# A hybrid decoder step on one core: convolution taps, mixers' weight loads and new latents moved in trace order

## The chip, the cores and the metric

The kernel runs on 1 core of one Trainium2 chip. The metric is the device time of one execution in microseconds (us). Before the change the median of 3 runs is 1201.39 us (1199.27 to 1204.67).

## The reference, cut to what matters

One layer of a decoder is computed for a prompt group (1 x 512 tokens and 16 learned meta tokens, 528 rows) and a sample group (8 sequences of 4 new tokens, 32 rows), with shared weights:

```python
h = x + 0.5 * swiglu(rmsnorm(x, ffn1_norm), ...)
z = rmsnorm(h, mix_norm) @ w_in          # -> q latent 256 | kv latent 256 | rope key 32 | conv input 2 x 512
a  = attention(q_lat, q_rope, c_kv, k_rope, w_uv)      # 8 heads over a compressed latent of 256
cv = silu(layernorm(depthwise_conv31(conv_in_a * sigmoid(conv_in_b)) + conv_b))
h = h + concat(rmsnorm(a), rmsnorm(cv)) @ w_out
h = h + 0.5 * swiglu(rmsnorm(h, ffn2_norm), ...)
```

Prompt attention is causal over the 528 rows. Each sample sequence attends to 4096 cached positions (32 pages of 128, found by a page table) and to its 4 new rows. The convolution is depthwise over 512 channels with 31 taps. The outputs are y of both groups, the new kv latents and rotary keys, and the last 30 rows of the convolution's input.

## The kernel before, in words

All activations are kept transposed, features on the 128 partitions and tokens (up to 560) along the free axis. A weight matrix streams in tiles; each is split into a high and a low part (`w_split`: ScalarE copies `wh` at L286, GpSimd subtracts `wl` at L287; where an FFN uses sums of weight blocks, VectorE subtracts at L300), and a product is made of three matmuls (`mm3`, L349).

On the chip the stages follow one another: the first FFN (to about 418 us), the input projections of the mixers (about 420 to 590), sample attention in 32 chunks of pages (about 446 to 733), prompt attention in 16 units (4 head pairs x 4 query tiles, about 591 to 731), the output projection (from about 741 to 787, first the convolution's four column groups, then attention's four), and the second FFN to the end. The convolution runs beside these: its taps from 460 to 640, its tail (mean, squares, norm, swish, second norm, split) from 640 to 741.

**How the order is made.** The kernel is written as coroutines that a small planner runs (`spawn`, `run`, L382 to 418). The planner has a clock of its own, in planned microseconds. A coroutine that yields a number advances this clock for everyone (0.715 for one `mm3` group of the projections, 1.6 for the scores of a chunk, 0.45 for its transposes, 1.05 for its products with the values). One that yields `Sleep(x)` is only not run before x has passed. One that yields an event waits for it. Where several can go on, the lowest priority number goes first: the convolution and the norms have 0, the two prompt workers 2, the main program 5. So the planner decides in which order instructions are traced. The framework then places each engine's instructions by readiness, with the traced order as priority, and from it come the order of each engine's queue and the buffers.

**Buffers.** Tiles of one tag share a set of buffers. The tag "t" has 10 (`Tm`): the probabilities `pr` and transposed probabilities of the prompt units, the squares `sq`, the tiles `th`, `cg`, `ot` are all of it. The rsqrt's work tiles "r" and "rr" have 1 each, its spread result "rb" 2. In PSUM the norms' sums take the banks "nr" and "cv". Weights' raw tiles `wr` have 3.

**The places of the change.**
- `conv_proc` (L917 for a tap): for each of 4 blocks of 128 channels, 31 operations on VectorE, one per tap, with a sleep of `TAP_PACE` after each; then ScalarE copies the sum to `acc` (L920) and GpSimd adds it to the sum over channels (L930). After the last block it spawns `conv_tail`.
- `conv_tail` (from L934): sleep `CS_LAT` (1.73); two halves of the mean on TensorE (L938), subtracted on VectorE (L941); four squares (L512) on ScalarE; sleep `CN_LAT` (8.16); a norm (`rsqrt_proc`: matmuls with ones L430, sqrt L462 and Newton's steps on VectorE L463 to L466, spread by L481, L483 and L485); per block the product by the norm (L953), tanh, bias, product (L958) and a square; sleep `CN_LAT` again; a second norm (its rsqrt on VectorE alone, L451 to L456); per block the product by gain and norm (L875) and the split into `mix` (L880 on ScalarE, L881 on GpSimd). Then `conv_done` is set.
- `w_split` and `w_dma` (L268 issues the load on SP's queue): after the split of tile j, loads are traced up to tile j + 4. A load waits in SP's queue until its buffer is free, that is until L287 has used the tile three loads earlier. SP also issues the page loads of the sample chunks (L1011).
- `latents_out` (L1497): when the scaled kv latents (`cc`, L818) are there, it stores them (L1501), transposes the samples' new latents on TensorE (L1504), copies them (L1505, L1506) and sets `new_ev`. `sample_proc` waits for `new_ev` at its chunk number 9 (L1144), for the scores against the new rows.
- `attn_norm` (from L1534): when the prompt workers and sample attention are done, four squares (L512, `sq<-at`), sleep 3.71, a norm, and the split of attention's half.
- The main program then waits for `conv_done` and does the convolution's half of the output projection for all 8 column groups, waits for attention's norm and does its half.

The planner's waits in these places, for reference:

```python
def rsqrt_proc(...):
    r0 = rsqrt(...)
    yield 0.3
    yield Sleep(RS_LAT)          # 4.05
    ...
    spread(rb, r0, site)
    yield 0.95
    ev.set(rb)
```

Of the kernel before, what the change touches and what calls it, by code (L numbers as in the profile page):

```python
# [52 lines left out]
CS_LAT = 1.73  # L53
CN_LAT = 8.16
AN_LAT = 3.71
TAP_PACE = 0.75

PAGE_TIME = 6.62

# [51 lines left out]
def kernel(  # L111
# [42 lines left out]
    def U(tag, shape, dt=F32, name="u"):  # L154
        return arena.tile(shape, dt, tag=tag, bufs=slots[tag], name=name)
# [24 lines left out]
    def SS(shape, name="ss", who="mm"):  # L180
        return ps_s.tile(shape, F32, tag=BANK_OF[who], bufs=BANKS[BANK_OF[who]], name=name)
# [29 lines left out]
    stream = []  # L211
# [3 lines left out]
    def add_w(ap, n):  # L215
        stream.append((ap, n))

    def add_ffn(gu, dn, apart=0, plain=NF):
        f0 = 0
        for nf in GROUPS:  # L220
            for f in range(f0, f0 + nf):
                if f == plain:
                    first_new.add(len(stream))
                add_w(gu[f], 2048 if f < plain else 0)
            for d in range(KD - (apart if f0 + nf == NF else 0)):
                add_w(dn[d, :, 128 * f0:128 * (f0 + nf)], 128 * nf)
            f0 += nf

    add_ffn(f1_gu, f1_d, 0, PLAIN1)
    for c in PLAN:  # L230
        for ap, n in {"q": [(w_in_t[0], 1024), (w_in_t[1], 1024)], 
                      "k": [(w_in_t[2], 1024)], "l": [(w_in_t[3], 1024)], "r": [(w_r_t, 512)],
                      "u": [(w_uq_t[0], 1024), (w_uq_t[1], 1024)]}.get(c) or [(w_in_t[4 + int(c, 16)], 1024)]:
            add_w(ap, n)
    add_w(w_uk_t, 1024)
    add_w(w_uv_t, 1024)
    for d, e in [(d, 1) for d in range(KD)] + [(d, 0) for d in range(KD)]:
        add_w(w_out_t[d, :, 512 * e:512 * e + 512], 512)
    add_ffn(f2_gu, f2_d, 2, PLAIN)


    subs = []
# [12 lines left out]
    def w_dma(upto):  # L255
        while st["dma"] < min(upto, len(subs)):
            i, c0, n = subs[st["dma"]]
            if n == 0:
                if c0 == 0:
                    raws[i, "a"] = []  # L260
                    for kh in range(2):
                        t = U("y" if i in first_new else "x", [128, 2, 512], F32, "ra")
                        nc.sync.dma_start(out=t, in_=stream[i][0][:, 1024 * kh:1024 * kh + 1024])
                        raws[i, "a"].append(t)
                st["dma"] += 1
                continue
            t = wpool.tile([128, n], F32, tag="wr", bufs=3, name="wr")
            nc.sync.dma_start(out=t, in_=stream[i][0][:, c0:c0 + n])  # L268
            raws[st["dma"]] = t
            dma_free[0] = max(dma_free[0], clock[0]) + n * WEIGHT_TIME  # L270
            st["dma"] += 1

    def w_split(upto):
        while st["split"] < min(upto, len(subs)):
            j = st["split"]
            n = subs[j][2]
            w_dma(j + 1)
            if n == 0:
                splits[j] = seven(*subs[j][0:2])
                st["split"] += 1  # L280
                w_dma(j + 8)
                continue
            raw = raws.pop(j)
            hi = wpool.tile([128, n], F32R, tag="wh", bufs=3, name="wh")
            lo = wpool.tile([128, n], F32R, tag="wl", bufs=3, name="wl")
            nc.scalar.activation(out=hi, in_=raw, func=AF.Copy)  # L286
            nc.gpsimd.tensor_tensor(out=lo, in0=raw, in1=hi.bitcast(F32), op=ALU.subtract)  # L287
            splits[j] = (hi, lo)
            st["split"] += 1
            w_dma(j + 4)  # L290

    def seven(i, m):

        a = raws[i, "a"]
        (a11, a21), (a12, a22) = [[t[:, j] for j in range(2)] for t in a]
        w = {0: a11, 4: a11, 5: a12, 6: a22}[m] if m in (0, 4, 5, 6) else raws[i, "s"]
        hi = wpool.tile([128, 512], F32R, tag="wh", bufs=3, name="wh")
        lo = wpool.tile([128, 512], F32R, tag="wl", bufs=3, name="wl")
        nc.scalar.activation(out=hi, in_=w, func=AF.Copy)  # L299
        nc.vector.tensor_tensor(out=lo, in0=w, in1=hi.bitcast(F32), op=ALU.subtract)  # L300

        if m == 0:
            raws[i, "s"] = U("y" if i in first_new else "x", [128, 512], F32, "ws")
        if m < 4:
            t = raws[i, "s"]
            out, x, y, op = [(t, a21, a22, ALU.add), (t, t, a11, ALU.subtract), (t, a12, t, ALU.subtract),
                             (a11, a11, a21, ALU.subtract)][m]
            last_sum[0] = nc.vector.tensor_tensor(out=out, in0=x, in1=y, op=op)  # L308
        if m == 3:
            raws.pop((i, "s"))  # L310
        if m == 6:
            raws.pop((i, "a"))
        return hi, lo

    class Weights:
# [7 lines left out]
        def at(self, c, n=128):  # L323
            j = self.j + c // 512
            c %= 512
            w_split(j + 1)
            hi, lo = splits[j]
            return hi[:, c:c + n], lo[:, c:c + n]

        def product(self, m):  # L330
            w_split(self.j + m + 1)
            return splits[self.j + m]

        def spent(self, m):
            splits.pop(self.j + m)
            w_split(self.j + m + 4)
# [547 lines left out]
    def conv_proc():  # L884

        last_tap = None
        for ct in range(4):
# [20 lines left out]
            for tp in range(CW):  # L908
# [7 lines left out]
                else:  # L916
                    last_tap = nc.vector.scalar_tensor_tensor(out=ps, in0=g[:, tp:S0 + tp], scalar=w, in1=ps,  # L917
                                                   op0=ALU.mult, op1=ALU.add)
                yield Sleep(TAP_PACE)
            nc.scalar.activation(out=a[:, 0:S0], in_=ps, func=AF.Copy)  # L920
# [394 lines left out]
    def main():  # L1315
# [176 lines left out]
        def latents_end():  # L1492
            yield from ev.drain()
            spawn(latent_finish(lat["c"], P_KV, c_ev), 0)
            spawn(latents_out(), 0)

        def latents_out():  # L1497
            yield c_ev
            cc = lat.pop("c")
            for j in range(2):  # L1500
                nc.sync.dma_start(out=kv_t[:, j], in_=cc[:, j])  # L1501
            ps = SS([32, 256], "cn")
            for kk in range(2):
                nc.tensor.transpose(out=ps[:, 128 * kk:128 * kk + 128], in_=cc[:, kk, NP:T], identity=ident)  # L1504
            nc.vector.tensor_copy(out=cn, in_=ps)  # L1505
            nc.vector.tensor_copy(out=ccs, in_=cc[:, :, NP:T])  # L1506
            yield 0.45
            new_ev.set()
# [268 lines left out]
```

## Time and profile before

| | us |
|---|---|
| median of 3 runs | 1201.39 |
| lowest and highest | 1199.27, 1204.67 |
| profiled execution | 1197.67 |
| span of its trace | 1195.9 |
| mean granted TensorE clock | 0.976 of full speed |
| busy: TensorE, VectorE, ScalarE, GpSimd | 1133.9, 792.3, 535.0, 379.2 |

The profiled execution's own time is 1.8 us longer than the span of its trace, from the first to the last instruction. In the rows further down, PE is TensorE's matmuls, PEld its weight loads, DVE VectorE, ACT ScalarE, POOL GpSimd, SP the engine whose queue (SPq) issues most DMAs. L12 is a line of the kernel, `out<-in` names the tiles, xN counts the instructions, and a bracket says how long the engine was idle before and what ended that. All times of rows count from the span's start.

### The profile page before, as it was taken

The numbers are of one execution on the slowest core, as the hardware profiler recorded it, in microseconds if no ns is written. First come the engines' busy times: TensorE is split into PE (matmuls) and PEld (weight loads), VectorE is DVE, ScalarE is ACT, GpSimd is POOL, SyncE is SP. The second block draws the span as 40 slices with busy tenths as digits, with TensorE's granted clock in tenths as the row PEclk, the third lists the DMA queues.
The fourth block names the chain that finished last, engine by engine and source line by source line (L and its number), as shares of the span: only waits on it lengthen the run. The fifth ranks groups of instructions, "written<-read, shape, count | busy, mean of one in ns | idle before, by whom it ended". The sixth has DMA issues, their size and how long they took to land.

```text
span 1195.9 us, 24540 instructions
## 1 busy us (share of the span) xinstructions
PE 1133.9 (95%) x9314; PEld 1032.3 (86%) x9314; DVE 792.3 (66%) x1537; ACT 535.0 (45%) x1119; POOL 379.2 (32%) x374
## 2 busy tenths in 40 slices
PE   7999999999999999987889999999899999999995
PEld 7989999999999987876545556999899999999994
DVE  6898138834884346999877465659981598168824
ACT  4445226533655414432534555444552355245631
POOL 5440420033004545577434323444214100410141
PEclk8999999999999989998979999999899999999997
DMA  4151322332226656987869884223233233323222
GB/s 159 63 167 61 108 65 84 107 111 78 89 74 211 199 175 196 305 262 232 272 224 315 308 286 158 80 89 98 89 125 90 68 106 102 101 66 104 67 69 75
DMA packets 91062, 168.60 MB, mean 141 GB/s; under 512 B 18976, under 2 KB 25120, under 8 KB 90944
## 3 DMA queue, kind: packets, MB, share of 16 engines
q1 hardware_dynamic: 88352, 162.27, 42.4%
q0 software_dynamic: 2048, 4.20, 1.2%
q8 instruction: 74, 1.21, 0.4%
q10 hardware_dynamic: 544, 0.56, 0.1%
q14 instruction: 44, 0.36, 0.1%
HBM read 161.33 MB, written 5.65 MB: 140 GB/s over the span
## 4 chain that ended last, share of the span: by engine, by line
PE 80%; DVE 10%; issue 3%; ACT 2%; DMA 2%; POOL 2%; SPq 0%; another core or an unknown queue 0%; DVEq 0%; POOLq 0%; ACTq 0%
PE mm L349 36%; PE mm L661 31%; PE sc L1045 3%; PE ob L1067 2%; PE po L1292 2%; PE s L1236 2%; DVE cacc L917 1%; PE pt L1276 1%; DVE xc L608 1%; POOL wl L287 1%; PE mm L1607 1%; DVE wl L300 1%; DMA out<-glu 1%; PE p L481 1%; DVE xt L627 1%
## 5 line engine op out<-in xcount | busy, mean ns | idle before, releaser
L287 POOL TENSOR_TENSOR wl<-wr,wh 128x512 fp32r<-128x512 f32 (+1 forms) x177 | 229.9, 1301 | 541.8 <-ACT wh L286 530.7
L661 PE MATMUL mm<-xc,wh 128*128 128x272 f32 (+1 forms) x1960 | 371.9, 290 | 1.1 <-ACT wh L299 0.9
L661 PEld LDWEIGHTS mm<-xc,wh 128*128 128x128 f32 x1960 | 306.6, 188 | 1.8 <-ACT wh L299 1.3
L661 PE MATMUL mm<-xc,wl 128*128 128x272 f32 (+1 forms) x980 | 281.5, 293 | 3.6 <-DVE wl L300 3.6
L349 PE MATMUL mm<-hid,wh 128*128 128x280 f32 (+1 forms) x1352 | 226.9, 289 | 1.8 <-ACT wh L286 1.8
L286 ACT ACTIVATE wh<-wr 128x512 fp32r<-128x512 f32 (+1 forms) x177 | 107.9, 612 | 251.7 <-PE mm L349 194.9
L349 PEld LDWEIGHTS mm<-hid,wh 128*128 128x128 f32 x1352 | 192.6, 188 | 2.0 <-ACT wh L286 2.0
L661 PEld LDWEIGHTS mm<-xc,wl 128*128 128x128 f32 x980 | 182.2, 188 | 9.8 <-DVE wl L300 9.8
L349 PE MATMUL mm<-xs,wh 128*128 128x280 f32 (+2 forms) x992 | 181.8, 303 | 8.5 <-DVE xs L543 3.5
L349 PEld LDWEIGHTS mm<-xs,wh 128*128 128x128 f32 (+1 forms) x992 | 150.5, 196 | 14.0 <-DVE xs L543 4.2
L782 DVE SCALAR_TENSOR_TENSOR h<-mm,h 128x280 f32<-128x280 f32 (+1 forms) x92 | 36.8, 441 | 165.9 <-PE mm L349 165.9
L349 PE MATMUL mm<-hid,wl 128*128 128x280 f32 (+1 forms) x676 | 140.9, 290 | 0.0
L349 PE MATMUL mm<-xs,wl 128*128 128x280 f32 (+2 forms) x496 | 114.3, 305 | 6.1 <-POOL wl L287 6.0
L299 ACT ACTIVATE wh<-ra 128x512 fp32r<-128x512 f32 x140 | 87.8, 629 | 71.5 <-PE mm L661 62.8
L349 PEld LDWEIGHTS mm<-hid,wl 128*128 128x128 f32 x676 | 106.4, 188 | 0.0
L300 DVE TENSOR_TENSOR wl<-ra,wh 128x512 fp32r<-128x512 f32 x140 | 99.7, 715 | 3.9 <-ACT wh L299 1.1
L299 ACT ACTIVATE wh<-ws 128x512 fp32r<-128x512 f32 x105 | 66.2, 630 | 76.5 <-DVE ws L308 36.3
L349 PEld LDWEIGHTS mm<-xs,wl 128*128 128x128 f32 (+1 forms) x496 | 83.2, 196 | 10.3 <-POOL wl L287 8.7
L300 DVE TENSOR_TENSOR wl<-ws,wh 128x512 fp32r<-128x512 f32 x105 | 73.7, 702 | 26.9 <-ACT wh L299 24.3
L917 DVE SCALAR_TENSOR_TENSOR cacc<-glu,par,cacc 128x512 f32<-128x512 f32 x120 | 89.9, 749 | 1.5
L998 POOL DMA_INDIRECT rope<-in_pool_r,pr_sb x64 | 63.7, 996 | 46.4 <-PE sc L1045 33.5
L668 ACT ACTIVATE sn<-mm 128x272 f32<-128x272 f32 (+1 forms) x105 | 40.9, 390 | 29.2 <-PE mm L661 29.2
(247 smaller groups left out, 1514.4 us busy)
## 6 DMA issues: line engine op xcount, KB each, us to landing
page<-in_pool_c SPq DMA_DIRECT2D x256, 256.0 KB
ra<-in_f_gu SPq DMA_DIRECT2D x70, 512.0 KB
wr<-in_f_d SPq DMA_DIRECT2D x62, 256.0 KB
wr<-in_f_gu SPq DMA_DIRECT2D x36, 256.0 KB
wr<-in_w_in_t SPq DMA_DIRECT2D x24, 256.0 KB
wr<-in_f_d SPq DMA_DIRECT2D x30, 192.0 KB
wr<-in_w_out_t SPq DMA_DIRECT2D x16, 256.0 KB
h<-in_x_t SPq DMA_DIRECT2D x8, 280.0 KB
```

Source lines behind the costliest of these rows:

```text
L286: nc.scalar.activation(out=hi, in_=raw, func=AF.Copy)
L287: nc.gpsimd.tensor_tensor(out=lo, in0=raw, in1=hi.bitcast(F32), op=ALU.subtract)
L299: nc.scalar.activation(out=hi, in_=w, func=AF.Copy)
L300: nc.vector.tensor_tensor(out=lo, in0=w, in1=hi.bitcast(F32), op=ALU.subtract)
L349: nc.tensor.matmul(out=ps[a][:m, 0:n], lhsT=w, rhs=x[:, a * n:(a + 1) * n], start=first and o == 0 and j == 0, stop=last and o == 1,)
L661: nc.tensor.matmul(out=ps, lhsT=w_[:, c], rhs=x, start=first and k == 0 and j == 0, stop=k == 3 and j == 2, skip_group_check=True)
L668: nc.scalar.activation(out=s, in_=src, func=AF.Copy)
L782: last = halves(lambda o, i, x: nc.vector.scalar_tensor_tensor(out=o, in0=i, scalar=0.5, in1=x, op0=ALU.mult, op1=ALU.add), hk(d), ps, hk( ...
L917: last_tap = nc.vector.scalar_tensor_tensor(out=ps, in0=g[:, tp:S0 + tp], scalar=w, in1=ps, op0=ALU.mult, op1=ALU.add)
L998: last = nc.gpsimd.indirect_dma_start(out=rope[:, pg], out_offset=None, in_=pool_r, in_offset=bass.IndirectOffsetOnAxis(ap=pr_sb[:, 32 * g ...
L1045: nc.tensor.matmul(out=ps[32 * b:32 * b + 32], lhsT=w[:, g, 32 * b:32 * b + 32], rhs=x, start=(i_ == 0), stop=(i_ == 2), tile_position=(0, ...
L1067: nc.tensor.matmul(out=ob[32 * b:32 * b + 32, :], lhsT=pts[:, 128 * pg + 32 * b:128 * pg + 32 * b + 32], rhs=tiles[b][:, pg, 0:256], start ...
```

## The change

Three places. The sleep after a tap becomes 1.4 in place of 0.75 planned us. The loads of the mixers' weights (input, query, key, value and output projections; `mixers` records their range in the stream; 49 loaded tiles) are traced up to tile j + 3 after the split of tile j, in place of j + 4. A sleep of 5 planned us stands before the stores and transposes of the new latents.

```diff
-TAP_PACE = 0.75
+TAP_PACE = 1.4
+CN_WAIT = 5.0
...
     add_ffn(f1_gu, f1_d, 0, PLAIN1)
+    mixers = [len(stream)]
...
         add_w(w_out_t[d, :, 512 * e:512 * e + 512], 512)
+    mixers = range(mixers[0], len(stream))
     add_ffn(f2_gu, f2_d, 2, PLAIN)
...
             st["split"] += 1
-            w_dma(j + 4)
+
+            w_dma(j + (3 if subs[j][0] in mixers else 4))
...
         def latents_out():
             yield c_ev
+            yield Sleep(CN_WAIT)
             cc = lat.pop("c")
```

## Rows read from the trace of the kernel before

**Rows 1.** The page, busy time of each engine over the whole span.
```profile
PE 1133.9 (95%) x9314; PEld 1032.3 (86%) x9314; DVE 792.3 (66%) x1537; ACT 535.0 (45%) x1119; POOL 379.2 (32%) x374
```

**Rows 2.** Windows: us, busy time (count) by engine, PEclk, DMA share, GB/s.
```profile
643.00:673.00 30.00, 29.00 (x303) 16.47 (x305) 15.19 (x65) 13.85 (x53) 11.06 (x21) 1.00 0.95 332
714.00:741.00 27.00, 23.43 (x327) 15.53 (x322) 13.44 (x49) 14.84 (x46) 7.08 (x9) 1.00 0.59 206
741.00:787.00 46.00, 45.26 (x361) 43.77 (x354) 29.84 (x55) 21.02 (x35) 19.61 (x15) 1.00 0.25 75
```

**Rows 3.** The tile cacc (the taps): durations min/median/max, first and last start.
```profile
L917 DVE SCALAR_TENSOR_TENSOR cacc<-glu,par,cacc x120: 674/751/757, 461.3 to 639.5; 128x512 f32<-128x512 f32 x120
...
L920 ACT ACTIVATE acc<-cacc x4: 597/598/599, 500.0 to 640.3; 128x512 f32<-128x512 f32 x4
```

**Rows 4.** Line 941 on DVE, same columns: subtraction of the mean.
```profile
L941 DVE TENSOR_TENSOR acc<-acc,mu x8: 419/430/431, 643.8 to 646.2; 128x272 f32<-128x272 f32 x8
```

**Rows 5.** ACT's timeline, 648 to 680: start, duration, instruction, idle before.
```profile
648.14 0.27 ACT L1281 ACTIVATE pr<-pt 48x128 f32<-48x128 f32 x1 [3.65 <-PE pt L1276]
...
672.74 0.60 ACT L1252 ACTIVATE pr<-s,mx 128x400 f32<-128x400 f32 x1 [0.20 <-DVE pr L1245]
...
673.33 2.28 ACT L512 ACTIVATE sq<-acc 128x544 f32<-128x544 f32 x4
...
678.63 1.28 ACT L462 ACT_TABLE_LOAD   x1
679.92 0.37 ACT L462 ACTIVATE r<-p,epsb 128x136 f32<-128x136 f32 x1
```

**Rows 6.** DVE's timeline, 690 to 755: the products by the rsqrt.
```profile
690.22 2.87 DVE L953 SCALAR_TENSOR_TENSOR acc<-acc,par,rb 128x544 f32<-128x544 f32 x4
...
712.77 0.72 DVE L958 SCALAR_TENSOR_TENSOR acc<-th,acc 128x544 f32<-128x544 f32 x1
...
728.20 0.78 DVE L875 SCALAR_TENSOR_TENSOR cg<-acc,par,rb 128x544 f32<-128x544 f32 x1 [1.03 <-ACT rb L483]
...
754.57 2.18 DVE L875 SCALAR_TENSOR_TENSOR at<-at,par,rb 128x544 f32<-128x544 f32 x3
```

**Rows 7.** The tile sq from 640 to 745.
```profile
L430 PE MATMUL p<-sq,ones_c x96: 276/279/306, 675.7 to 742.5; 128*32 128x136 f32 x96
L512 ACT ACTIVATE sq<-acc x8: 642/648/658, 673.3 to 713.7; 128x544 f32<-128x544 f32 x8
L512 ACT ACTIVATE sq<-at x4: 647/656/657, 737.4 to 740.1; 128x544 f32<-128x544 f32 x4
```

**Rows 8.** The tile pr (prompt units' probabilities): the last exponential.
```profile
L1252 ACT ACTIVATE pr<-s,mx x36: 369/481/597, 606.9 to 721.5; 128x264 f32<-128x264 f32 x16, 128x400 f32<-128x400 f32 x8, 128x144 f32<-128x144 f32 x6, 128x272 f32<-128x272 f32 x6
```

**Rows 9.** PE's timeline: the stalled transposes, and the last chunk.
```profile
548.28 0.39 PE L1504 MATMUL cn<-cst,cc 128*32 128x128 f32 x1 [4.71 <-DVE cc L818]
...
733.15 1.07 PE L1067 MATMUL ob<-page,pts 128*32 128x256 f32 x16
```

**Rows 10.** Windows around that stall, columns as in rows 2.
```profile
540.00:548.00 8.00, 2.92 (x42) 1.52 (x42) 7.95 (x14) 2.19 (x6) 7.16 (x9) 0.79 1.04 378
548.00:552.00 4.00, 3.72 (x18) 3.72 (x19) 4.00 (x8) 1.34 (x2) 0.99 (x1) 0.56 1.05 378
```

**Rows 11.** SP's queue: what its DMA issues waited for, 400 to 760.
```profile
SPq L268 <- POOL wl L287: 69.6, 20, 14.7
SPq L1011 <- PE ob L1067: 36.2, 12, 11.2
```

**Rows 12.** Waits of ACT from 420 to 600.
```profile
ACT wh L286 <- DMA wr<-in_w_in_t: 10.5, 4, 6.3
```

**Rows 13.** ACT's timeline, 740 to 742: attention's last square, table load.
```profile
740.12 0.66 ACT L512 ACTIVATE sq<-at 128x544 f32<-128x544 f32 x1
740.79 1.28 ACT L462 ACT_TABLE_LOAD   x1
```

**Rows 14.** POOL's timeline, 728 to 745: the conv group's last products.
```profile
736.87 4.28 POOL L881 TENSOR_TENSOR mix<-cg,mix 128x544 fp32r<-128x544 f32 x3 [5.10 <-ACT mix L880]
```

## The prediction

> **What bounds the kernel now.** I read the page first: TensorE is busy 95% of the span [rows 1], so a change of order can win only where TensorE waits, and can lose wherever it makes TensorE wait. The three edits act between 420 and 790 us (input projections, the two attentions, the convolution, the output projection), so next come the windows of the late part [rows 2]. TensorE does 29.0 of 30 us at 643 to 673, 23.4 of 27 at 714 to 741 and 45.3 of 46 at 741 to 787. The attentions fill TensorE until about 741, and then the output projection fills it. That second fill exists because two things end together: sample attention, whose last product runs at 733.15 [rows 9] and whose squares end at 740.12 + 0.66 = 740.78 [rows 13], and the convolution's normalised result, ready at 736.87 + 4.28 = 741.15 [rows 14]. The convolution half of the projection starts on the latter and hides attention's norm, which is done only from 754.57 on [rows 6].
>
> So the number to look for is when the convolution's result is ready. Its 124 taps run from about 460 to 640 on VectorE [rows 3], its mean is subtracted by 646.2 + 0.43 = 646.6 [rows 4], but its squares run only at 673.33 [rows 5]. Between, ScalarE had an idle gap of 3.65 us before 648.14, and the squares come directly behind the exponential of a prompt unit that started at 672.74 [rows 5]. The squares share a tag of ten buffers ("t") with the prompt units' tiles, and I read this as tiles of one tag getting buffers in the order in which they were traced: work traced later cannot fill an earlier gap, even with its data there. What a change of trace order does to the convolution's tail is therefore the question.
>
> **Taps further apart (TAP_PACE).** No instruction is added; 124 sleeps of the planner grow from 0.75 to 1.4 plan us. A tap can only be traced at a step boundary of the plan. One chunk period of the plan is 0.45 (transposes), 0.715 (one projection step), 1.05 (products), 1.6 (next scores) and 4 x 0.715, in all 6.675. From its start, a pace of 0.75 finds a boundary at 1.165, 2.215, 3.815, 5.245 and 6.675: 5 taps a period. At 1.4 it is 2.215, 3.815, 5.245 and 6.675: 4 taps. 124 taps then need 31 instead of 24.8 periods, 207 instead of 166 plan us. Followed through all steps, those of the prompt units included, the first block starts at 416 and the taps end at 578 before and at 634 after. Sample attention ends at 633 in the plan of before, and the convolution's result is ready at 636, as on the chip: together. After the change the tail's squares are traced 1.73 + 2 x (0.48 + 1.5) = 5.7 later than the last tap, at about 640. That is behind every prompt unit (the last ends at 622) and behind sample attention's end (633, or 638 with the new wait of 5). The plan's own sleeps for the rest of the tail put the result at 634 + 43 = 677 at least.
>
> On the chip the taps fill gaps of VectorE and end at about 640 as now. The tail does not: its squares come behind the last tiles of the units and the squares of attention, which end at 740.8 less the time d by which sample attention ends earlier. From there:
> - Two norms, attention's and the convolution's first, with one buffer each for the rsqrt's work tiles. Alone they take 740.78 to 754.57 = 13.8 [rows 6, 13] and 675.61 (673.33 + 2.28) to 690.22 = 14.6 [rows 5, 6]. Bounds: side by side 14.6, in sequence 28.4. I take 20, since only the rsqrt's vector work excludes the other's.
> - Scale, tanh and swish to the last square: 690.22 to 713.7 + 0.65 = 714.35 [rows 6, 7], 24.1 with prompt units between. VectorE's own work is three operations on each of four blocks at 0.72 [rows 6], 8.6. Bounds 9 and 24; I take 11.5, near the low end, as no unit is left to interleave.
> - Second norm: 714.35 to 728.20 = 13.9 [rows 6, 7] beside the last chunks. Bounds 10 and 14; I take 12.
> - Gain and split: 0.78 [rows 6] + 0.65 for a copy of a square's size [rows 7] + 4 x 1.43 on GpSimd (4.28 for 3) [rows 14] = 7.2; I take 7.
>
> Together 50.5 (bounds 41 and 73), so the result is ready at 791.3 - d where it was at 741.15: 50.1 - d later. Nothing covers it. The conv half of the projection is first in trace order, and TensorE has nothing else to do from the end of sample attention on. What is late next is the projection as a whole: its two halves then follow at once, as now.
>
> **What d is.** The tail's work leaves the stretch in which TensorE is full: 64 of the 96 ones-matmuls at 0.279 [rows 7], 17.9 if none overlapped, 4.4 if four run side by side; I take 5. The other part is the third edit. d is 10, between 0 and 22.
>
> **Later transposes of the new latents (CN_WAIT).** Moved later in trace order are two stores of latents on SP's queue, two transposes, two copies and the event that sample attention needs at chunk 9. In before the transposes hold TensorE's queue for 4.71 us, waiting for VectorE's scaling [rows 9]; TensorE is busy 2.92 of 8 us there [rows 10]. Traced behind other matmuls they wait for nothing. Worth 4.7 at most, as the engine then meets the full stretch earlier, down to 0 if the samples' new-key scores wait instead. I take 4.7, as the wait ends once, and it is in d. The two stores have no waiting reader; what is queued behind them on SP is page loads, which go first now.
>
> **Weight loads one split later (w_dma).** 49 loads move by one split. Now, with three buffers, the load traced four ahead waits in SP's queue for a low-part subtraction that is traced later: 69.6 us over 20 waits, the longest 14.7 [rows 11], with page loads behind it. Moved later it waits for a subtraction traced just before. No load can start before its buffer is free, so the cost is only lead time lost: ScalarE waited 10.5 us in 4 times for these loads [rows 12], and at worst that doubles. The page loads themselves mostly wait for chunks' products (36.2 us) [rows 11], so earlier issue buys little. Bounds: a gain of 5, a loss of 10.5; I take 0, since both waits lie beside a TensorE that is full.
>
> **Cold start.** [...] I take 1, bounds 0 and 2. [...]
>
> A norm also needs a table load on ScalarE: 1.28 us, with the square root at 679.92, directly behind it [rows 5]. [...]
>
> **The sum.** 50.1 - 10 + 0 + 1 = +41. The profiled execution took 1197.67 (span 1195.9), so 1238.7. That execution lies 3.7 under the median of the three runs, 1201.39, and that much of doubt is in the range. Forecast 1239. With most bounds at their low ends it is about 1216, with most at their high ends about 1262; this is the likeliest case's own range.
>
> **Rivals.**
> A, faster. Buffers don't follow trace order; the squares waited at 646.6 to 673.3 for something else. Then the taps still end near 640, the tail still runs as a filler, and sample attention alone sets the end. The gain is the 4.7 of the transposes' stall plus about 2 of queue waits: 1191. It decides for this case if the squares run before about 700. For it: the taps have slack of 100 us. Against it: the gap of 3.65 us that the squares did not use [rows 5]. 14%.
> B, slower but by less. The squares are held only by the last prompt unit, whose last exponential starts at 721.5 [rows 8]. From 722: 2.3 of squares, 14.6, 13, 12 and 7 give 771, less d 761, against 741.15: +20, 1218. It decides if the squares come before attention's own. The margin in the plan is only 2 us (638 against 640), which is for it. 20%.
> C, no change. The edits only reorder priorities: the pace is already 1.30 plan us on average (161 over 124), so little moves, and the stall of the transposes comes back as a wait of the new-key scores. 1201. 8%.
> The forecast proper, +41, keeps 58%.
>
> **How the numbers follow.** A measurement of this kernel tells some 0.5%, 6 us, from no change. Faster 0.14 (A), same 0.08 (C), slower 0.78 (forecast and B). The range holds the forecast, B and C, and leaves out A and the far end above 1262: 1196 to 1262.
>
> **What would show it.** Right: the convolution's squares at 725 or later instead of 673.33, in one group near attention's squares; TensorE all but idle for some 40 us before the first product of the projection, waiting for the conv group's copies; windows after that as before. The last tap still near 640, and no 4.71 before the transposes. B shows as squares at 722 to 730, ahead of attention's. A shows as squares before 700 and a projection that starts at about 735. If the squares are late and yet the time is not, another stage bounded this one and the whole reading is wrong; if the last tap itself moves past 680, the plan's pace rules VectorE more than I take it to.

## The result and the profile after

The changed kernel takes 1239.49 us (median of 4, 1234.77 to 1244.14) beside 1200.56 for the kernel before, now the median of four runs (1199.27 to 1204.67). The ratio is 1.0318, with a 95% interval of 1.027 to 1.0366: slower, by 39 us. The forecast was 1239 in a range of 1196 to 1262. The traced execution has a span of 1233.0 where before had 1195.9, so 37.1 us have to be found in the rows.

First the windows of the late part, as in [rows 2], with one more behind them (us, busy time and count by engine, the granted clock, DMA share, GB/s):

```profile
643.00:673.00 30.00, 27.53 (x283) 15.29 (x282) 12.94 (x54) 13.27 (x51) 15.15 (x24) 1.00 0.90 318
...
714.00:741.00 27.00, 15.54 (x218) 9.52 (x214) 7.08 (x20) 10.59 (x26) 0.68 (x2) 0.67 0.31 115
741.00:787.00 46.00, 20.81 (x156) 17.14 (x149) 25.91 (x53) 14.69 (x25) 10.08 (x7) 0.60 0.04 12
787.00:830.00 43.00, 43.00 (x350) 42.70 (x348) 22.04 (x41) 19.66 (x31) 18.55 (x14) 1.00 0.28 90
```

At 643 to 673 TensorE's busy time has hardly changed. Then it does 15.5 of 27 us and 20.8 of 46, where it did 23.4 and 45.3, and from 787 on it is full. That is 7.9 + 24.5 = 32 us less busy time in two lines, at a mean granted clock of 0.60 to 0.67 where the kernel before had 1.00 [rows 2].

ScalarE's timeline says what that stretch is (start, duration, instruction, idle before). Lines of the new source stand 3 to 5 below those of the old: the squares are L516, the sqrt L466.

```profile
730.80 0.66 ACT L516 ACTIVATE sq<-at 128x544 f32<-128x544 f32 x1
731.37 2.28 ACT L516 ACTIVATE sq<-acc 128x544 f32<-128x544 f32 x4
733.66 1.28 ACT L466 ACT_TABLE_LOAD   x1
734.95 0.37 ACT L466 ACTIVATE r<-p,epsb 128x136 f32<-128x136 f32 x1
...
749.57 1.28 ACT L960 ACT_TABLE_LOAD   x1
...
761.82 0.66 ACT L516 ACTIVATE sq<-acc 128x544 f32<-128x544 f32 x1 [1.39 <-DVE acc L962]
```

The convolution's squares, at 673.33 before [rows 5], start at 731.37, directly behind attention's last one (730.80). Two more rows show that they waited neither for data nor for a busy ScalarE: the mean is subtracted by 676.4 + 0.44 = 676.8, 54.5 us earlier, and ScalarE is idle several times between, for 3.82 us before 716.58.

```profile
L945 DVE TENSOR_TENSOR acc<-acc,mu x8: 430/431/439, 674.0 to 676.4; 128x272 f32<-128x272 f32 x8
```
```profile
716.58 0.47 ACT L1030 ACTIVATE p<-sc,nm 128x256 f32<-128x256 f32 x1 [3.82 <-DVE p L1025]
```

VectorE, GpSimd and TensorE show the rest of the chain: attention's products by its norm, the convolution's first products (L957), the second ones (L879), the last split, the first matmuls of the projection.

```profile
739.99 2.87 DVE L879 SCALAR_TENSOR_TENSOR at<-at,par,rb 128x544 f32<-128x544 f32 x4
...
749.73 2.87 DVE L957 SCALAR_TENSOR_TENSOR acc<-acc,par,rb 128x544 f32<-128x544 f32 x4
...
769.69 3.96 DVE L879 SCALAR_TENSOR_TENSOR cg<-acc,par,rb 128x544 f32<-128x544 f32 x4
```
```profile
771.25 6.25 POOL L885 TENSOR_TENSOR mix<-cg,mix 128x544 fp32r<-128x544 f32 x4 [48.80 <-ACT mix L884]
```
```profile
738.16 0.48 PE L485 MATMUL p<-rr,unit 2*128 2x136 f32 x2 [5.97 <-DVE rr L448]
...
771.22 1.27 PE L353 MATMUL mm<-mix,wh 128*128 128x272 f32 x4 [2.01 <-ACT mix L884]
```

The convolution's result is ready at 771.25 + 6.25 = 777.50, where it was at 741.15 [rows 14]: 36.35 us later. The span is 37.1 us longer, so that is the loss but for 0.75. TensorE's bracket before 738.16, 5.97 us idle until VectorE's `rr`, recurs at the other two norms (5.96 us before 747.93, 4.62 before 767.82): it waits for a chain on the other engines that nothing covers.

Two rows answer to [rows 3] and [rows 9]: the taps, and the new latents' transposes.

```profile
L921 DVE SCALAR_TENSOR_TENSOR cacc<-glu,par,cacc x120: 674/752/757, 456.9 to 620.8; 128x512 f32<-128x512 f32 x120
```
```profile
550.25 0.39 PE L1509 MATMUL cn<-cst,cc 128*32 128x128 f32 x1 [3.80 <-DVE cc L822]
```

The last tap starts at 620.8, 18.7 us earlier than before. The wait in front of the transposes is 3.80 us, hardly less than the 4.71 it should have lost.

### The profile page after: what moved, and what is told of

It is laid out like the page before. It is cut to its first block, busy times and chain, and to the rows that moved or that the text cites. A ratio compares the mean times of both kernels' runs of the same rounds, so it can differ in the third digit from the quotient of the medians.

```text
span 1233.0 us, 24555 instructions
## 1 busy us (share of the span) xinstructions
PE 1144.1 (93%) x9314; PEld 1038.3 (84%) x9314; DVE 788.6 (64%) x1537; ACT 537.1 (44%) x1119; POOL 374.9 (30%) x374
## 5 line engine op out<-in xcount | busy, mean ns | idle before, releaser
L353 PE MATMUL mm<-hid,wh 128*128 128x280 f32 (+1 forms) x1352 | 228.0, 291 | 1.8 <-ACT wh L289 1.8
L353 PEld LDWEIGHTS mm<-hid,wh 128*128 128x128 f32 x1352 | 193.8, 189 | 2.0 <-ACT wh L289 2.0
L353 PE MATMUL mm<-xs,wh 128*128 128x280 f32 (+2 forms) x992 | 180.8, 301 | 7.7 <-DVE xs L547 3.8
L353 PEld LDWEIGHTS mm<-xs,wh 128*128 128x128 f32 (+1 forms) x992 | 148.8, 194 | 13.9 <-DVE xs L547 4.5
L353 PE MATMUL mm<-hid,wl 128*128 128x280 f32 (+1 forms) x676 | 141.5, 291 | 0.0
L353 PE MATMUL mm<-xs,wl 128*128 128x280 f32 (+2 forms) x496 | 112.8, 302 | 8.0 <-POOL wl L290 7.9
L353 PEld LDWEIGHTS mm<-hid,wl 128*128 128x128 f32 x676 | 106.8, 189 | 0.0
L303 ACT ACTIVATE wh<-ws 128x512 fp32r<-128x512 f32 x105 | 66.2, 630 | 76.5 <-DVE ws L312 37.1
L353 PEld LDWEIGHTS mm<-xs,wl 128*128 128x128 f32 (+1 forms) x496 | 82.1, 194 | 12.1 <-POOL wl L290 11.0
```

Source lines behind the costliest of these rows:

```text
L353: nc.tensor.matmul(out=ps[a][:m, 0:n], lhsT=w, rhs=x[:, a * n:(a + 1) * n], start=first and o == 0 and j == 0, stop=last and o == 1,)
```

## The experiments

Theory T: the tail's tiles get buffers, and its norm the work tiles, in trace order; so the pace's effect is the place of the tail in trace order, and the time follows from when the convolution's result is ready against sample attention's end. Rival 1: another of the three edits carries the loss. Rival 2: the later taps themselves do, or the plan's pace as such, evenly with its size. Each run is compared with runs of the kernel before on the same chip; those had medians of 1200 to 1201 us, but 1189.4 for the runs warm_tail, pace_05 and own_075, so ratios are what can be compared across runs.

### pace_only: the first edit alone

```diff
-TAP_PACE = 0.75
+TAP_PACE = 1.4
```

> The kernel before with the pace of 1.4 alone. If the order of the convolution's tail is the whole cost, the tail's squares run behind attention's squares (near 731 to 741) and the time is 1236 to 1246, as the changed kernel's 1239 or a little over it. If the weight loads or the later transposes carry part of the loss, it is below 1230.

Measured: 1238.17, ratio 1.0312 (1.029 to 1.0334). The tile sq from 640 to 800 (durations min/median/max, first and last start):

```profile
L512 ACT ACTIVATE sq<-acc x8: 635/652/656, 735.0 to 765.4; 128x544 f32<-128x544 f32 x8
L512 ACT ACTIVATE sq<-at x4: 657/659/660, 732.1 to 734.4; 128x544 f32<-128x544 f32 x4
```

The convolution's first square (735.0) again stands behind attention's last (734.4). The pace alone gives the whole loss (1.0312 beside 1.0318); rival 1 falls.

### two_and_three, wdma_only, cn_only: the other edits

In two_and_three the pace of the changed kernel is put back to 0.75. The other two add one edit each to the kernel before:

```diff
-            w_dma(j + 4)
+            w_dma(j + (3 if subs[j][0] in mixers else 4))
```
```diff
             yield c_ev
+            yield Sleep(5.0)
```

> The changed kernel with the pace put back to 0.75, so the later weight loads and the later transposes alone. If the tail's order is the whole cost: 1195 to 1203, its squares at 665 to 690. If the later weight loads starve the projections: 1208 or more, with ScalarE's waits for weights at 420 to 600 above 20 us.

> The kernel before with the mixers' loads traced one split later, nothing else. Forecast's value: 0, so 1197 to 1204. The rival that earlier page loads are worth something: 1190 to 1195; that lost lead costs: 1206 to 1212.

> The kernel before with the later transposes of the new latents alone. By the forecast the 4.71 us wait ahead of the transposes goes and sample attention ends 4 to 5 us earlier: 1195 to 1198. If the wait only hides another (TensorE waits for the same scaling in VectorE elsewhere): 1199 to 1203, with a wait of 3 to 5 us left in front of the transposes.

Measured: both 1196.84, ratio 0.9952 (0.9936 to 0.9967); the loads alone 0.9982 (0.9961 to 1.0003); the transposes alone 0.997 (0.9946 to 0.9994). So the two edits without the pace are faster than either kernel, by 0.5%, and the two parts add up to it within their intervals. The rows of two_and_three: the transposes, and the window in which the kernel before had 2.92 of 8 us busy [rows 10].

```profile
547.94 0.28 PE L1509 MATMUL cn<-cst,cc 128*32 128x128 f32 x1 [0.62 <-DVE cc L822]
```
```profile
540.00:548.00 8.00, 7.25 (x75) 5.40 (x73) 7.21 (x15) 3.13 (x9) 6.28 (x8) 1.00 0.85 242
```
```profile
L516 ACT ACTIVATE sq<-acc x8: 657/660/662, 680.0 to 720.0; 128x544 f32<-128x544 f32 x8
...
L516 ACT ACTIVATE sq<-at x4: 640/656/658, 739.0 to 741.4; 128x544 f32<-128x544 f32 x4
```

The wait shrank to 0.62 and TensorE is busy 7.25 of the 8 us. Yet attention's last square starts at 741.4, no earlier than the 740.1 of before [rows 7]. The stall's removal is real in its window and not to be seen at sample attention's end in these traces. This trace is of the slowest of its six runs (1200.73), but the one of cn_only (1196.35, near its median) says the same: a wait of 2.12 us before the transposes, and attention's last square at 740.3. Where the 0.5% comes in stays open.

### own_buffers: the late pace, with the tail freed

The pace stays at 1.4. The tail's squares, tanh tiles and gain products are written into the convolution's used-up input tiles and its channel sum, instead of tiles of tag t; attention's norm is traced behind the tail's second norm.

```diff
-        s = [square(acc(ct)) for ct in range(4)]
+        own = [csum[0]] + [glu_t[ct][:, 0:NQ] for ct in range(1, 4)]
+        for ct in range(4):
+            nc.scalar.activation(out=own[ct], in_=acc(ct), func=AF.Square)
...
-            t = Tm([128, NQ], "th")
+            t = own[ct]
...
-            for e in p_done + [s_done]:
+            for e in p_done + [s_done, conv_n2]:
```

> The changed kernel, pace 1.4 kept; the tail's squares, tanh tiles and gain products go into the convolution's own used-up input tiles in place of tag t, and attention's norm is traced behind the tail's second norm. If buffers and work tiles in trace order hold the tail: its squares run soon after the mean, at 640 to 690, the result is ready before 741 and the time is 1190 to 1202. If the later taps themselves are the cost (the plan's pace, or a late mean): 1225 or more.

Measured: 1199.34, ratio 0.9993 (0.9973 to 1.0013). Three of the four squares (into `glu`; the first, into the channel sum, starts at 681.26), the last split, and attention's squares:

```profile
L953 ACT ACTIVATE glu<-acc x3: 639/639/641, 681.8 to 682.9; 128x544 f32<-128x544 f32 x3
```
```profile
732.35 4.46 POOL L887 TENSOR_TENSOR mix<-glu,mix 128x544 fp32r<-128x544 f32 x3
```
```profile
L516 ACT ACTIVATE sq<-at x4: 646/658/660, 744.2 to 747.9; 128x544 f32<-128x544 f32 x4
```

With the same pace and the same taps, the squares run 50 us earlier, directly behind the mean, the result is ready at 732.35 + 4.46 = 736.81, and the loss is gone. That bears theory T out, though tiles and the norms' order were changed together. Rival 2 falls: with the same taps, the ratio is within 0.0041 of that of two_and_three, which has the old pace, where the pace had cost 0.0366. What the new tiles cost or save by themselves is not told apart in this. Attention's last square, 747.93 + 0.66, now ends 7.8 us later than before. The tail's work sits again in the stretch in which TensorE is full, which would explain it but was not tested.

### own_first: the first step of the tail freed

As own_buffers, but only the first four squares have own tiles, and attention's norm is traced behind the tail's first norm instead of its second.

```diff
-            for e in p_done + [s_done]:
+            for e in p_done + [s_done, conv_n1]:
```

> As own_buffers, but only the tail's first squares are in own tiles and attention's norm is traced behind the tail's first norm; tanh tiles still take buffers of tag t. If trace order of buffers holds: squares at 640 to 690, the first tanh only behind attention's squares near 732, result ready some 18 us before the changed kernel's 777.7, time 1217 to 1226. If squares alone were held: 1205 or less.

Measured: 1227.16, ratio 1.0217 (1.0186 to 1.0248), just beyond the upper end of what was expected. The products before the tanh, attention's last square, the tanh tiles (still of tag t), and the end of the tail:

```profile
L966 DVE SCALAR_TENSOR_TENSOR acc<-acc,par,rb x4: 780/781/785, 705.6 to 708.1; 128x544 f32<-128x544 f32 x4
```
```profile
740.78 0.66 ACT L516 ACTIVATE sq<-at 128x544 f32<-128x544 f32 x1
```
```profile
L969 ACT ACTIVATE th<-acc,hlb x4: 732/732/748, 741.3 to 751.0; 128x544 f32<-128x544 f32 x4
```
```profile
765.94 6.22 POOL L887 TENSOR_TENSOR mix<-cg,mix 128x544 fp32r<-128x544 f32 x4 [33.87 <-ACT mix L886]
```

The squares ran at 679.9, like those of own_buffers. The products were done by 708.9, but the first tanh came at 741.3, right behind attention's squares (these ended at 741.4); in own_buffers, with own tiles, it ran at 708.4. That is the same rule, one step further on. From the end of attention's squares to the result it is 772.16 - 741.44 = 30.7 us, 15.3 less than the changed kernel's 777.50 - 731.46 = 46.0. Of this only 5.3 arrives, because sample attention ended 10.0 later; that part had been left out of the expectation. These 5.3 us compare the slowest run here with the fastest of the changed kernel; by the medians it is some 12 us (1.0217 beside 1.0318).

### pace_10 and pace_11: the step in the pace

```diff
-TAP_PACE = 1.4
+TAP_PACE = 1.0
```

(1.1 in pace_11.)

> The changed kernel with a pace of 1.0. By the plan's step boundaries a chunk period still takes 5 taps, as at 0.75, so nearly no loss: 1198 to 1208. If the loss grows evenly with the pace: 0.25 of 0.65, some 15 us, 1215.

> The changed kernel with a pace of 1.1. By the step boundaries a chunk period takes 4 taps, as at 1.4, so most of the loss: 1220 to 1240, the squares near the last prompt units (715 to 725). If the loss grows evenly with the pace: 0.35 of 0.65, 1221; then it is told apart only by the run at 1.0.

Measured: 1202.26, ratio 1.0025 (1.0004 to 1.0046), and 1226.09, ratio 1.0202 (1.0168 to 1.0235). The trace of pace_11 is of the slowest of its four runs, 1236.15. The convolution's squares at 1.0 and at 1.1, with those after the swish as the last start:

```profile
L516 ACT ACTIVATE sq<-acc x8: 646/652/660, 691.7 to 727.3; 128x544 f32<-128x544 f32 x8
```
```profile
L516 ACT ACTIVATE sq<-acc x8: 646/663/677, 723.9 to 763.4; 128x544 f32<-128x544 f32 x8
```

Between these two runs, a tenth of a planned microsecond moves the first square by 32 us in the traces and costs 24 (medians, same chip), 0.0177 of the ratio. In the trace of pace_11 the squares come ahead of attention's, yet the first tanh starts at 748.17, right behind attention's last square at 747.60: the tail is held one step later, as in own_first. From 0.75 to 1.0 the ratio grew by 0.0073 (0.9952 of two_and_three to 1.0025), and from 0.75 to 1.4 by 0.0366 (to 1.0318). Growing evenly, that would be 0.0056 for a tenth and 0.0141 at 1.0. So the greater part comes in a step, where the hand count over a chunk period turns from 5 taps to 4; a smaller part does grow before it. That pace_11 stays below 1.4 (1.0202 beside 1.0318), with 4 taps in both, was not taken apart.

### pace_05 and own_075: is there more to gain

The changed kernel with a pace of 0.5; own_buffers with a pace of 0.75.

> The changed kernel with a pace of 0.5, both other edits kept. The convolution's result is then traced ready ahead of sample attention's end. If the tail being just in time still costs TensorE something at 714 to 741 (23.4 of 27 us busy in the kernel before): 1188 to 1195. If TensorE is full up to sample attention's end anyway and the work is only moved: 1194 to 1200, as with 0.75.

> own_buffers with the pace at 0.75, both other edits kept. If the tail is off the path already with 0.75: as two_and_three, 1194 to 1200. If freeing it from tag t gains more: 1188 to 1193.

Measured: ratio 1.0009 (0.9988 to 1.003) and 1.0139 (1.0107 to 1.0172). In pace_05 the first square runs at 639.6 and the result is ready at 711, 30 us early, and that buys nothing:

```profile
714.00:741.00 27.00, 23.84 (x269) 19.98 (x265) 6.21 (x18) 9.92 (x23) 6.95 (x7) 0.94 0.41 142
741.00:787.00 46.00, 42.37 (x321) 41.30 (x320) 30.24 (x53) 21.40 (x37) 15.75 (x13) 0.93 0.22 72
```

TensorE's 23.8 and 42.4 us are together 66.2, beside 68.7 before [rows 2]: the projection's matmuls (L353) have moved forward, 16.4 us of them at 714 to 741 in place of 3.9, and nothing is won. The alternative in which an early tail gains 5 us or more falls; but the ratio, some 1202 us at the usual 1200.56, is above the other range too. Against two_and_three (0.9952) a pace of 0.5 even gives the gain of the other edits back; why was not taken apart. own_075 is slower than either alternative had it, with attention's last square starting at 750.0. Its projection takes 12.7 us of 714 to 741, less than in pace_05, where attention's last square starts at 737.8; so that early projection work crowds out sample attention does not explain it by itself, and the cause stays open. Neither beats two_and_three, which stays the fastest version here.

### warm_tail and warm_tied: the price of the cold start

Idle matmuls were put into the tail to raise TensorE's clock there. In the changed kernel its low level was a granted 0.50 at 731 to 771, where a ones-matmul took 0.434 us beside 0.279 before [rows 7]; at 771 to 781, where the projection starts, 0.66 was granted. In warm_tail they read only constants:

```diff
+        if site in (4, 5):
+            warm(12)
...
             s.append(square(a))
+            warm(6)
```

> The changed kernel with 48 idle matmuls of ones put between the tail's steps (12 behind the sums of each of its two norms, 6 behind each of its four blocks), so that TensorE is not at its low level when the projection starts; the result is unchanged. If the low level costs the 1 us that the forecast gave it: 1237 to 1241. If it is worth the difference between 0.434 and 0.279 us per ones-matmul and some 0.15 us for each of the projection's first 50 to 60 matmuls, as the changed kernel's trace suggests: 1229 to 1235. Should the added matmuls delay the tail's own: above 1241.

Measured: ratio 1.0403 (1.037 to 1.0437). As they depended on nothing, they ran before 726, ahead of the tail, and the clock at 731 to 771 stayed at 0.50: the run says nothing on its question. By its time it would be the case in which the matmuls delay the tail, but from the end of attention's squares to the result it is 46.1 us, as without them. In warm_tied they read the tail's own squares (12 and 3 in place of 12 and 6).

> The changed kernel with 36 idle matmuls that read the tail's squares, so that they can run only in the tail: 12 behind the sums of each of its two norms, 3 behind each of its four blocks; the result is unchanged. If the low level costs the forecast's 1 us: the ratio to the kernel before stays within 0.004 of the changed kernel's 1.0318, with TensorE's granted clock at 771 to 781 above the 0.66 of the changed kernel. If the low level costs 4 us or more: ratio 1.028 or lower. If the matmuls hold up the tail's own: above 1.035.

Measured: ratio 1.0355 (1.0324 to 1.0386). The stretch of the tail in the changed kernel, and in warm_tied:

```profile
731.00:771.00 40.00, 8.94 (x96) 4.31 (x88) 25.00 (x54) 15.84 (x28) 0.00 (x0) 0.50 0.00 1
```
```profile
731.00:771.00 40.00, 21.40 (x208) 16.91 (x206) 22.74 (x49) 16.79 (x31) 0.00 (x0) 0.71 0.00 1
```
```profile
774.58 6.24 POOL L892 TENSOR_TENSOR mix<-cg,mix 128x544 fp32r<-128x544 f32 x4 [48.76 <-ACT mix L891]
```

The mean clock there rose from 0.50 to 0.71, but at 771 to 781 it was 0.70 beside 0.66, so the projection still started at a low clock and the price of that stays unmeasured. One thing it does show: from the end of attention's squares (733.67 + 0.66) to the result (774.58 + 6.24) it is still 46.5 us, beside 46.0. A higher clock did not make the tail shorter, though the added matmuls may have taken back what it gave. So the ratio above 1.035 does not come from a longer tail, which had been named for it; attention's squares end 2.9 later than in the changed kernel, and why is open.

## Why the prediction was right, point by point

**What bounds.** Right. The loss is the time by which the convolution's result comes later than before, 36.35 of 37.1 us; it stands 46.0 us behind the end of sample attention, where the two used to end together.

**Trace order and buffers.** Right. With the same pace, own tiles and attention's norm traced behind the tail's, there is no loss (own_buffers); with only the first tiles freed, the next ones of tag t wait (own_first). Both runs changed tiles and the norms' order together, so no run shows the tiles by themselves, and the norms' work tiles were not tested alone. Against the traced order holding instructions without the buffers speaks that the squares in own tiles ran as soon as their data was there, at 680 to 682, though they are traced at the same place as in the changed kernel, by the hand count behind all prompt units; and that in own_first ScalarE was idle for 3.81 us before 726.26, with the first tanh's data there since 706.3 (705.56 + 0.78).

**The planner's count.** Right where it was tested: the step between 1.0 and 1.1 is where a chunk period loses a tap by the hand count. The plan's own times (634, 638, 640) were not read from a run. Rival A (tail as a filler) is out with the squares at 731.37; rival C with the ratio; rival B is out because the squares stood behind attention's own, though pace_11, with its first square at 723.9, is what B described (at +20; it cost 24).

**The terms.** Two norms: 731.46 to 749.73 = 18.3 (20 was taken). Swish: 749.73 to 761.82 + 0.66 = 12.75 (11.5). Second norm: 762.48 to 769.69 = 7.2 (12, bounds 10 and 14). Gain and split: 769.69 to 777.50 = 7.8 (7). In all 46.0 in place of 50.5. The one that was mis-sized is the second norm, below its bounds. The row it was taken from has work of the last chunks and prompt units between its steps: there the rsqrt on VectorE took 6.1 us (716.79 to 722.93) and the spread 5.1 (723.03 to 728.17), here 4.5 and 1.8 (763.27 to 767.77, 767.82 to 769.58), with nothing else between.

**d.** 740.78 - 731.46 = 9.3, where 10 was taken, but not from its parts as stated. The step "Traced behind other matmuls they wait for nothing" failed: the wait was 3.80 in the changed kernel and 2.12 with this edit alone (cn_only); only with the load edit at the old pace did it shrink to 0.62. What the tail's ones-matmuls take together shows in the timeline of before: 1.69 us for 32 from 675.74 on, and 0.44, 0.44, 0.44 and 0.41 for eight each, 3.4 for the 64 that the prediction bounded by 4.4 and 17.9. With the pace alone, d is 740.78 - (734.43 + 0.66) = 5.7, which fits the tail's work leaving the full stretch (5 was taken), though no run shows that share by itself. The other 3.6 cannot be given to the transposes: at the old pace they gave no earlier end (two_and_three), and in warm_tied, which has all three edits, attention's squares end 2.9 later than in the changed kernel. Single traces scatter by about as much as that rest.

**The weights.** Taken as 0, measured 0.9982 with an interval that reaches 1.0003: right within what can be told.

**What else missed.** The last tap was expected near 640 and started at 620.8. It gained nothing: the mean, subtracted by 646.6 before, came 30 us later, its first matmul at 673.3. It had to wait for the channel sum (GpSimd, 670.14), and this for the last block's four new rows: their products `win` (L905), also tiles of tag t, ran at 664.70, where they ran at 613.54 before. The prediction left these tiles out; that their buffers held them is likely by the same rule, but not tested. It cost nothing here, as the squares were held until 731.

**The cold start.** 1 was taken, and no run shows this term. What the trace of the changed kernel showed in its place is a granted clock of 0.66 at 771 to 781, where the projection starts, and a span that grew by 0.75 more than the result's delay. That leaves no room for a much larger price, but it was not measured by itself.

That the forecast of 1239 fell within a microsecond of the median is partly luck: the terms were 4.5 too long and d 0.7 too large, so that the sum missed the traced execution (1234.77) by 3.9, and that execution happens to lie 4.7 under the median of its four.

## What to carry to other kernels

Where instructions and buffers follow the order in which they are traced, a sleep in the planner is no delay but a place in that order: find which later work the moved part will stand behind, and price the chain from there with nothing to cover it. Pacing acts in steps, because a coroutine is resumed only at the boundaries of other work; count the boundaries before tuning the number. Beside a full engine, work that was ready 30 us early gained nothing here, and work that was ready 36 us late, after the engine had run dry, cost the whole delay.

## What the runs showed of the hardware

In the changed kernel the last of VectorE's four products by gain and norm (the tile cg) ran from 771.78 on beside GpSimd's first two subtractions of the last split (mix) and took 1.868 us, where the other three took about 0.78. Those two subtractions took 1.817 and 1.829, the two behind them 1.363 and 1.362:

```profile
L879 DVE SCALAR_TENSOR_TENSOR cg<-acc,par,rb x4: 780/782/1868, 769.7 to 771.8; 128x544 f32<-128x544 f32 x4
```
```profile
L885 POOL TENSOR_TENSOR mix<-cg,mix x4: 1362/1590/1829, 771.2 to 776.1; 128x544 fp32r<-128x544 f32 x4
```

So 1.868 is 0.78 and about one more microsecond, and the subtractions with no product beside them were the shorter ones. The third product, which ended only after the first subtraction had started at 771.25, still took 0.780. That the last product and the subtractions held each other up is the author's reading of these times, and no run tested it.

The table loads on ScalarE took 1.28 us here too, as in [rows 5], with the next operation directly behind them: the sqrt at 734.95 behind the load of 733.66, and the tanh at 750.86 behind the load of 749.57.
